# An MLP block on one core: where the sums of new weight blocks stand in superblock 1, and another fixed order for the first and last pair of later first matmuls

## The chip, the core and the metric

The kernel runs on one core of a Trainium2 chip. The core has a matrix engine (TensorE, "PE" in the profile; its weight loads are shown apart as "PEld"), a vector engine (VectorE, "DVE"), a scalar engine (ScalarE, "ACT"), a general engine (GpSimd, "POOL") and a sync engine (SyncE, "SP") that here issues DMA transfers. Each engine works through its own queue in order, and the engines wait for each other by semaphores. The metric is the device time of one execution in microseconds; less is better. Three runs of the kernel before gave 1500.38, 1503.52 and 1505.25 us.

## The reference

```python
def setup_inputs():
    batch, seq_len, hidden_dim = 8, 1024, 1024
    intermediate_dim = 4 * hidden_dim
    ...

def reference(x, w1, w2):
    h = x @ w1
    h = 0.5 * h * (1 + np.tanh(np.sqrt(2 / np.pi) * (h + 0.044715 * h ** 3)))
    return (h @ w2).astype(np.float32)
```

x has 8192 rows of 1024, w1 is 1024 x 4096, w2 is 4096 x 1024, all float32; the kernel multiplies in float16 and accumulates in float32.

## The kernel before

**Superblocks and matmuls.** The 8192 rows are taken in eight superblocks of 1024. Each has a first matmul (x times w1, then GELU, into g) and a second one (g times w2, into the output). Both use Strassen's scheme in Winograd's form: each operand is cut into four quarters, and seven products of quarters or of sums of quarters take the place of eight. The sums of the weights are `W_SUM` (numbers 5, 6, 7, 4; numbers 1, 2, 3 are plain quarters), the sums of the other operand `S_SUM`. From superblock 2 on some of the seven products are themselves cut once more in the same way; those are called inner products, and their sums inner sums.

**What superblocks 0 and 1 do besides.** w1 is worked on in four blocks ("quads", class `MadeQuad`) of two pairs each. Superblock 0 reads the weights, casts them and keeps the plain blocks in memory. Superblock 1 reads a plain block back (four loads of 512 KB on SP's queue, L201), makes its four sums on DVE (`sum`, L236) and stores each on POOL's queue (L246), and makes the inner sums of products 1 and 2 (`STORED_1`; four jobs each, `inner_jobs`, L252, stored at L270). It also makes the inner sums ("splits") of two products of the second matmul's w2 (`split_in_m1`, L1124: two loads on SP at L1130, four sums on DVE, four stores of 256 KB on POOL at L1141). Superblocks 2 to 7 only read all this back (`StoredHalf`, L296; loads at L318), except for the inner sums of products 3 and 5, which POOL makes (`make_sums`, L320, L329).

**The first matmul, `matmul1_seeded` (L754).** It runs over eight pairs of column chunks, j = 0 to 7. The order of all its work is written out by hand in tables: each entry is an operation and a number, its due place in thousandths of a pair; the entries of all pairs are merged by 1000 j + number (L946) and given out in that order, which fixes the order on every engine. `ORDER_PLAIN` serves every pair of superblock 1, `ORDER_HEAD` the first, `ORDER_TAIL` the last and `ORDER` the other pairs of superblocks 2 to 7. The entries are:

- `Pmch` with m the product, c the chunk and h the half: an outer step, two matmuls of 512 columns; `Pmrk` is step k of an inner product, two matmuls of 256 columns (L825, L832; the matmul itself is L821).
- `a`, `b`, `p5`: copies on ACT out of a PSUM bank (`move`, L876). `w`, `v`: additions on DVE of the copy p5 to bank A. `acc_`, `q11_`, `q12_`, `q2x_`: additions on DVE that put an inner product's parts together and into a bank (`add`, L853). PE writes into that bank next, so it waits for them.
- `gbch`: GELU on ACT (L892). After both gelus of blocks 11 and 21 POOL subtracts them (L903).
- `J`: a slot for jobs on DVE. It has room 1.2, and takes jobs from the pair's list until their costs have used it up (L805).

**The jobs.** In superblock 1 `Two.__init__` fills the list with what `ahead(j)` returns and with the splits that were set aside for this pair. In superblocks 2 to 7 pair 0 has the inner sums of x (`xs.inner_jobs`, four jobs of cost 0.42 per product) for those of products 1, 5, 2, 3 that the second matmul before hasn't made: eight jobs in superblock 2, twelve in the others. The operands that a `StoredHalf` loads, and their order on SP's queue, follow the order in which the table names its products (`operands_of`, L285).

All DVE operations have the line L152 in the profile, ACT's copies L168. Tiles named u come from one pool of 26 buffers, gc from one of 4, ps are the eight PSUM banks.

Of the kernel before, what the change touches and what calls it, by code (L numbers as in the profile page):

```python
# [21 lines left out]
SUMS = tuple(W_SUM)  # L22
# [2 lines left out]
INNER_1 = (1, 5, 2, 3)  # L25
STORED_1 = (1, 2)
SPLIT_IN_M1 = (2, 3)
SPLIT_AT = (0, 2, 4, 6)


def slots(table):
# [30 lines left out]
def order(text):  # L62
    return [(int(n), o) for o, n in (token.split(":") for token in text.split())]
# [4 lines left out]
    P2c00:511 P2c10:513 P2c01:526 P3c10:550 J:556 P3c00:564 P3c01:616 J:672 P7c00:704 P7c10:715  # L68
    P7c01:777 P7c11:817 P2c11:825 P3c11:825 g120:841 v0:852 v1:858 P4c00:871 P4c01:877 g111:883 g220:894
    P4c10:900 g110:904 P4c11:908 g121:1064 g210:1076 g211:1145 g221:1725""")  # L70
ORDER_HEAD = order("""J:-1385 P1c10:-1332 P1c11:-1168 J:-1152 P1c00:-1041 P1c01:-1039 a1:-953 P2r5:-773 a0:-627 P2r1:-592
    P5c00:-480 P5c10:-400 P5c01:-302 P6c00:-240 P6c01:-196 J:-160 P6c10:-111 J:-106 p50:170 acc_2:211
    q11_2:227 P2r6:278 P5c11:303 J:330 P6c11:342 w0:343 P3c00:354 q12_2:356 J:405 P3c01:417 p51:429
    P2r7:431 w1:433 P2r3:468 g120:488 q2x_2:504 P7c00:540 P2r2:577 J:584 J:690 P7c01:737 v0:792 J:827
    P2r4:841 g110:853 P7c10:856 P7c11:865 P3c10:953 v1:954 P4c00:982 g111:1052 P3c11:1079 J:1130 J:1151
    P4c01:1171 J:1211 g121:1215 g210:1320 P4c10:1380 P4c11:1511 g220:1571 g211:1653 g221:1719""")
ORDER = order("""P1r5:-255 P1r1:-201 q11_1:-134 P1r2:-80 s5_1:-76 P1r6:-72 P5r5:-7 q12_1:6 P5r1:10 P1r7:18 P1r3:20
    q11_5:166 s5_5:184 P5r2:194 P5r6:195 q2x_1:195 P1r4:203 a0:204 P2r5:204 q12_5:225 P6c00:229 P5r7:236
    a1:249 P5r3:277 P2r1:284 P6c01:320 q2x_5:387 q11_2:393 P6c10:398 P2r6:398 P5r4:403 P2r2:404 P3r5:408
# [1 line left out]
    P7c01:644 P3r6:653 P2r3:677 q2x_2:677 P7c10:680 acc_3:712 q12_3:729 g110:805 P2r4:810 P7c11:818  # L81
    v0:828 P3r7:857 P3r2:908 q2x_3:914 P3r3:924 P4c00:952 g111:994 v1:1049 g120:1106 P4c01:1111
    P3r4:1166 g121:1208 P4c10:1329 g210:1333 P4c11:1490 g220:1512 g211:1541 g221:1555""")
ORDER_TAIL = order("""P1r5:-319 P1r1:-290 s5_1:-54 q11_1:-44 P1r6:-31 q12_1:-17 P5r5:58 P5r1:105 P1r7:121 q11_5:124
    P1r2:134 s5_5:187 q2x_1:198 P5r2:203 P1r3:253 P5r6:266 P1r4:310 P2r5:319 a0:321 q12_5:357 P5r7:372
    P2r1:376 P5r3:389 q2x_5:389 P6c00:390 a1:398 P6c01:414 P5r4:415 P6c10:420 P6c11:434 q11_2:475
    acc_2:477 p50:505 P3r5:508 P3r1:508 P2r6:519 p51:523 w0:559 P7c00:563 w1:569 q11_3:643 P7c01:650
    q12_2:660 P3r6:666 v0:679 P7c10:684 P2r2:705 acc_3:734 P3r2:742 P2r3:782 P7c11:814 P4c00:868
    q12_3:880 P2r7:918 P3r7:922 v1:989 q2x_3:1011 P4c01:1063 P4c10:1110 q2x_2:1124 P4c11:1186 P3r4:1299
    P3r3:1390 P2r4:1431 g220:1455 g110:1463 g221:1715 g210:1802 g211:1864 g121:1875 g111:1922 g120:2446""")  # L90


@with_exitstack
def kernel(
# [11 lines left out]
    _, I = w1.shape  # L106
    _, O = w2.shape
# [5 lines left out]
    NI = I // P // 2  # L113
    OH = O // 2
    NQ = HT // P
    QC = 4
# [637 lines left out]
    def matmul1_seeded(xs, sb, quads):  # L754
        g = {b: gp.tile([P, NI, HT], GT, name=f"g{b}") for b in ("11", "12", "21", "22")}
        plain = sb == 1
        npair = NI // 2
# [4 lines left out]
        splits = {}  # L762

        def table(j):
            if plain:
                return ORDER_PLAIN
            return ORDER_HEAD if j == 0 else ORDER_TAIL if j == npair - 1 else ORDER

        class Two:
            def __init__(self, j):  # L770
                self.j, self.cs = j, (2 * j, 2 * j + 1)
                names = [o for _, o in table(j)]
                self.left = len(names)
                self.inner = [m for m in range(1, 8) if f"P{m}r1" in names]
                self.banks, self.temp, self.z = {}, {}, {}
                self.jobs, self.done = [], set()
                if plain:
                    self.source = quads[j // 2]
                    self.jobs = ahead(j) + splits.pop(j, [])
                    return  # L780
                for i in range(len(quads), min(j + 3, npair)):
                    quads.append(StoredHalf(i, table(i)))
                self.source = quads[j]
                if j == 0:
                    quads[0].make_sums()
                if j < npair - 1:
                    quads[j + 1].make_sums()
                if j == 0:
                    for m in INNER_1:
                        if m not in xs.inner:  # L790
                            pool = (gcp, "gc") if m in (1, 5) else (up, "u")
                            self.jobs += [(0.42, job) for job in xs.inner_jobs(m, *pool)]
# [119 lines left out]
        def ahead(j):  # L912

            q, second = divmod(j, 2)
            jobs = []
            if j < 2:
                jobs += quads[0].inner_jobs(STORED_1[j])
            if j in SPLIT_AT:
                i = SPLIT_AT.index(j)
                splits[j + 1] = [(0.7, job) for job in split_in_m1(SPLIT_IN_M1[i // 2], i % 2)]  # L920
            if q == NI // QC - 1:
                return jobs
            if not second:
                quads.append(MadeQuad(q + 1, False, True))
            quad = quads[q + 1]
            jobs += [(1.2, lambda m=m: quad.sum(m, pin=True)) for m in ((7, 4) if second else (5, 6))]
            jobs += quad.inner_jobs(STORED_1[second])
            return jobs

        def steady(j):  # L930

# [46 lines left out]
    def matmul2_made(sb, g, keep_w1, xb):  # L978
# [98 lines left out]
        for m, name, first in (  # L1077
# [3 lines left out]
            for q in range(NQ):  # L1081
# [12 lines left out]
                if (m, q) == (4, 0) and sb:  # L1094
                    quad = StoredHalf(0, ORDER_HEAD)
                if (m, q) == (1, NQ - 1) and sb == 0:
# [27 lines left out]
    def split_in_m1(m, h):  # L1124

        raw, t = [], {}
        for k in range(2):
            raw.append(gcp.tile([P, 2, HALF], DT, name="gc"))
            q = 2 * k + h
            nc.sync.dma_start(out=flat(raw[k]), in_=stored(w2_d[q], raw2_d[q], m))  # L1130

        def make(i, n):
            u, op, v = W_SUM[n]
            if i % 2 == 0:
                t["two"] = gcp.tile([P, 2, HALF], DT, name="gc")
            t[n] = t["two"][:, i % 2]
            in0, in1 = (
                t[b] if isinstance(b, int) else raw[int(b[0]) - 1][:, int(b[1]) - 1] for b in (u, v)
            )
            tt(t[n], in0, in1, op, True)  # L1140
            nc.gpsimd.dma_start(  # L1141
                out=in_d[m][:, i, h * QC:(h + 1) * QC, :].rearrange("p c n -> p (c n)"), in_=t[n]
            )

        return [lambda i=i, n=n: make(i, n) for i, n in enumerate(SUMS)]
# [175 lines left out]
    xs, quads = first.xs, [first.quad]  # L1321
    for sb in range(NSB):
# [4 lines left out]
        if sb < 2:  # L1327
            xs, quads = matmul2_made(sb, g, None if sb else quads[-1].keep_raw, nxt)
            continue
        matmul2(sb, g, early, nxt)  # L1330
        if nxt is not None:
            xs, quads = nxt, [StoredHalf(0, ORDER_HEAD)]

# [29 lines left out]
```

## Time and profile before

| | |
|---|---|
| median of three runs | 1503.52 us (1500.38 to 1505.25) |
| the profiled execution | 1499.09 us; its span 1497.3 us |
| granted TensorE clock, mean | 0.994 |
| first matmul of superblock 1 | from 208.50 to 315.57 us |
| its second matmul | to 412.27 us |
| first matmul of superblock 2 | from 412.27 to 503.21 us |
| its second matmul | to 588.86 us |
| first matmul of superblock 3 | from 588.86 to 682.60 us |
| DMA traffic | 452.23 MB, mean 302 GB/s |

The span is what lies between the first and the last instruction of the profiled execution. A line of the timeline gives the start and the length in us, the engine and source line, the operation, what it writes and reads, its tile, how many instructions were merged, and in brackets how long the engine had been idle before and what ended that. "issue" is time in which an engine waited for nothing that the profile shows. The ends of matmuls are modelled, since they are pipelined.

### The profile page before, as it was taken

Reading aid. Unit: us, or ns where it says so; the run is one execution under the profiler, and the core shown is the slowest. Engines: PE = TensorE matmul, PEld = TensorE weight load, DVE = VectorE, ACT = ScalarE, POOL = GpSimd, SP = SyncE. Lnnn points to the kernel's source line nnn. Section 1 sums busy time; section 2 is a strip of 40 time slices with the busy share of each in tenths; the row PEclk is TensorE's granted clock in tenths of the full one; section 3 lists DMA queues with packets and bytes.
Section 4 is the critical chain, followed back from the end, with each engine's and each line's share of the span. In section 5 each row is a group of like instructions: output and inputs, shape, how many; then the busy total and the mean of one; then the engine's idle time right before and its main releaser. Section 6 shows DMA issues by size and latency. Waiting matters only on the chain.

```text
span 1497.3 us, 27850 instructions
## 1 busy us (share of the span) xinstructions
PE 1467.9 (98%) x10347; PEld 1011.6 (68%) x10347; DVE 1169.4 (78%) x1672; ACT 606.7 (41%) x1210; POOL 560.1 (37%) x703
## 2 busy tenths in 40 slices
PE   8999989999999999999999999999999999999998
PEld 5444434444466787668866688666886678856787
DVE  5657348557867999779977799778997789877897
ACT  5665015531066411673126721267214662057510
POOL 2442124332377111861037611475115731157211
PEclk9999999999999999999999999999999999999999
DMA  9999898797897899969999699996999969996896
GB/s 324 339 360 404 203 383 293 261 316 250 332 288 211 271 349 351 333 186 362 351 321 305 169 371 337 357 276 198 391 299 352 275 190 378 324 350 215 301 310 198
DMA packets 241864, 452.23 MB, mean 302 GB/s; under 512 B 80576, under 2 KB 85696, under 8 KB 240832
## 3 DMA queue, kind: packets, MB, share of 16 engines
q1 hardware_dynamic: 214816, 357.12, 68.8%
q0 software_dynamic: 26912, 93.34, 21.1%
q8 instruction: 81, 1.33, 0.3%
q14 instruction: 55, 0.45, 0.1%
HBM read 353.89 MB, written 111.15 MB: 311 GB/s over the span
## 4 chain that ended last, share of the span: by engine, by line
PE 79%; DVE 4%; DMA 1%; issue 1%; SPq 0%; DVEq 0%
PE ps L821 40%; PE ps L1192 33%; PE ps L1233 6%; DVE u L152 2%; DMA u<-w_d 1%; DVE gc L152 1%; DVE tmp L152 0%; DVE ps L152 0%; SPq L318 0%; DVEq L152 0%
## 5 line engine op out<-in xcount | busy, mean ns | idle before, releaser
L821 PE MATMUL ps<-u 128*128 128x256 f16 (+1 forms) x3508 | 627.6, 328 | 20.4 <-DVE ps L152 20.4
L821 PEld LDWEIGHTS <-u 128*128 128x128 f16 x4180 | 411.2, 98 | 262.1 <-issue 33.7
L152 DVE TENSOR_TENSOR tmp<-tmp,ps 128x512 f32<-128x512 f32 x352 | 238.1, 685 | 127.6 <-PE ps L821 50.3
L1192 PE MATMUL ps<-u,gc 128*128 128x256 f16 x2688 | 300.3, 273 | 0.0
L168 ACT COPY tmp<-ps 128x512 f32<-128x512 f32 x282 | 163.8, 588 | 309.6 <-PE ps L821 150.8
L1192 PEld LDWEIGHTS <-gc 128*128 128x128 f16 x2688 | 262.9, 98 | 30.6 <-issue 0.2
L152 DVE TENSOR_TENSOR u<-u 128x2048 f16<-128x2048 f16 (+3 forms) x292 | 226.9, 818 | 26.4 <-DMA raw_d<-u 11.9
L892 ACT ACTIVATE g<-ps 128x512 f16<-128x512 f32 x336 | 197.9, 601 | 106.4 <-PE ps L821 105.8
L329 POOL TENSOR_TENSOR u<-u 128x256 f16<-128x256 f16 x336 | 216.4, 670 | 51.6 <-DMA u<-w_d 19.5
L1192 PE MATMUL ps<-u,g 128*128 128x256 f16 x2016 | 227.9, 273 | 0.0
L976 POOL DMA_DIRECT2D out_dram<-u x70 | 64.0, 960 | 432.0 <-DVE u L152 231.3
L168 ACT COPY u<-ps 128x512 f32<-128x512 f32 (+1 forms) x134 | 78.0, 587 | 347.2 <-PE ps L1192 340.4
L1192 PEld LDWEIGHTS <-g 128*128 128x128 f16 x2016 | 197.3, 98 | 22.8
L152 DVE TENSOR_TENSOR ps<-tmp,ps 128x256 f32<-128x256 f32 (+1 forms) x298 | 154.7, 532 | 38.4 <-PE ps L821 30.8
L903 POOL TENSOR_TENSOR g<-g,g 128x1024 f16<-128x1024 f16 x56 | 122.0, 2179 | 159.2 <-ACT g L892 159.1
L152 DVE TENSOR_TENSOR u<-u,ps 128x512 f32<-128x512 f32 x216 | 147.7, 684 | 36.5 <-PE ps L1192 27.9
L1233 PE MATMUL ps<-u,g 128*128 128x512 f16 x768 | 166.4, 379 | 0.0
L152 DVE TENSOR_TENSOR ps<-seed,ps 128x256 f32<-128x256 f32 (+1 forms) x168 | 94.5, 563 | 71.7 <-PE ps L821 69.3
L1233 PEld LDWEIGHTS <-g 128*128 128x128 f16 x768 | 75.1, 98 | 90.7
L821 PE MATMUL ps<-gc,u 128*128 128x256 f16 x672 | 120.4, 273 | 0.0
L152 DVE TENSOR_TENSOR gc<-g,gc 128x2048 f16<-128x2048 f16 x84 | 114.0, 1357 | 3.1 <-PE ps L1192 3.1
L152 DVE TENSOR_TENSOR gc<-g 128x2048 f16<-128x2048 f16 x78 | 95.1, 1220 | 0.0
(50 smaller groups left out, 741.6 us busy)
## 6 DMA issues: line engine op xcount, KB each, us to landing
u<-w_d SPq DMA_DIRECT2D x336, 256.0 KB, 6.6
u<-in_d SPq DMA_DIRECT2D x168, 512.0 KB, 7.9
u<-raw_d SPq DMA_DIRECT2D x252, 256.0 KB, 6.9
out_dram<-u POOLq DMA_DIRECT2D x70, 512.0 KB, 9.4
gc<-in_w_dram SPq DMA_DIRECT2D x48, 512.0 KB, 6.0
u<-in_d SPq DMA_DIRECT2D x90, 256.0 KB, 6.3
raw_d<-u SPq DMA_DIRECT2D x32, 512.0 KB, 8.5
u<-raw_d SPq DMA_DIRECT2D x32, 512.0 KB, 13.4
```

Source lines behind the costliest of these rows:

```text
L152: i = nc.vector.tensor_tensor(out=out, in0=in0, in1=in1, op=op)
L168: tc.keep_in_program_order(nc.scalar.copy(out=out, in_=in_))
L329: tc.keep_in_program_order(nc.gpsimd.tensor_tensor(out=operand(j), in0=operand(u), in1=operand(v), op=op))
L821: tc.keep_in_program_order(nc.tensor.matmul(out, lhsT=w, rhs=x, start=first, stop=True, skip_group_check=not first,))
L892: gelu_last[0] = nc.scalar.activation(out=g[b][:, self.cs[h], :], in_=src, func=GELU)
L903: nc.gpsimd.tensor_tensor(out=g["21"][:, cs], in0=g["11"][:, cs], in1=g["21"][:, cs], op=SUB)
L976: return nc.gpsimd.dma_start(out=rows, in_=src, **kw)
L1192: tc.keep_in_program_order(nc.tensor.matmul(bank[:, i * OH // 2:(i + 1) * OH // 2], lhsT=t[:, c, i * P:(i + 1) * P], rhs=self.y[j][:, c, : ...
L1233: tc.keep_in_program_order(nc.tensor.matmul(pair(bank), lhsT=a[:, c, :], rhs=chunks(pieces[c // QC])[:, :, c % QC, :], start=(first and c ...
```

## The change

Two things change. First, in superblock 1 the jobs are handed out differently. Before, pair j of a quad q made two of the four sums of the next quad (5 and 6 in the first pair, 7 and 4 in the second) and the inner sums of one stored product of it, and pairs 0 and 1 also made those of quad 0. After, the first pair of quad q makes the eight inner jobs of quad q itself (cost 0.8 each, so two to a slot), and the second pair makes all four sums of the next quad (one to a slot). The plain blocks are still loaded at the first pair of the quad before. The splits of w2 are loaded in pairs 1, 3, 5, 7 instead of 0, 2, 4, 6; they are made one pair after their load, and the last ones in pair 7 itself, where five empty jobs fill the five slots before them.

Second, `ORDER_HEAD` and `ORDER_TAIL` are other tables with the same operations, except that the head has four slots J instead of eleven, all of them late.

```diff
-SPLIT_AT = (0, 2, 4, 6)
+SPLIT_AT = (1, 3, 5, 7)
...
-ORDER_HEAD = order("""J:-1385 P1c10:-1332 P1c11:-1168 J:-1152 P1c00:-1041 P1c01:-1039 a1:-953 P2r5:-773 a0:-627 P2r1:-592
-    P5c00:-480 P5c10:-400 P5c01:-302 P6c00:-240 P6c01:-196 J:-160 P6c10:-111 J:-106 p50:170 acc_2:211
-    q11_2:227 P2r6:278 P5c11:303 J:330 P6c11:342 w0:343 P3c00:354 q12_2:356 J:405 P3c01:417 p51:429
-    P2r7:431 w1:433 P2r3:468 g120:488 q2x_2:504 P7c00:540 P2r2:577 J:584 J:690 P7c01:737 v0:792 J:827
-    P2r4:841 g110:853 P7c10:856 P7c11:865 P3c10:953 v1:954 P4c00:982 g111:1052 P3c11:1079 J:1130 J:1151
-    P4c01:1171 J:1211 g121:1215 g210:1320 P4c10:1380 P4c11:1511 g220:1571 g211:1653 g221:1719""")
+ORDER_HEAD = order("""P5c00:-1464 P2r5:-1229 P2r1:-1036 P1c10:-843 P1c11:-781 P1c00:-759 a1:-684 P1c01:-618 P5c10:-615
+    P5c01:-608 a0:-563 P5c11:-508 p50:-437 P6c10:-298 p51:-221 P6c11:-112 q11_2:-26 acc_2:-10 P6c00:41
+    w1:296 P2r6:411 P6c01:431 q12_2:466 P7c10:480 w0:511 P2r7:512 P7c11:542 q2x_2:548 v1:569 P2r2:622
+    P3c00:627 P2r3:640 J:652 g110:726 P2r4:745 P7c00:762 g221:778 P7c01:783 v0:785 P3c01:806 P4c10:833
+    J:913 P4c11:924 g111:937 P4c00:1006 P3c10:1017 P3c11:1026 g120:1046 g220:1078 J:1129 P4c01:1202
+    g121:1207 g210:1229 J:1337 g211:1528""")
...
-ORDER_TAIL = order("""P1r5:-319 P1r1:-290 s5_1:-54 q11_1:-44 P1r6:-31 q12_1:-17 P5r5:58 P5r1:105 P1r7:121 q11_5:124
...
-    q12_3:880 P2r7:918 P3r7:922 v1:989 q2x_3:1011 P4c01:1063 P4c10:1110 q2x_2:1124 P4c11:1186 P3r4:1299
-    P3r3:1390 P2r4:1431 g220:1455 g110:1463 g221:1715 g210:1802 g211:1864 g121:1875 g111:1922 g120:2446""")
+ORDER_TAIL = order("""P1r5:-249 P1r1:-200 s5_1:-147 q11_1:-70 P1r6:-70 q12_1:-37 P5r5:13 P5r1:48 P1r7:111 s5_5:170
...
+    P7c11:927 P7c01:954 P3r2:1060 v1:1155 P3r3:1164 g111:1166 v0:1218 P3r7:1237 P4c10:1247 g221:1254
+    g220:1306 P4c11:1309 g120:1341 P4c00:1667 q2x_3:1799 P4c01:1874 g211:1889 P3r4:1926 g210:2235
+    g121:2960""")
...
             q, second = divmod(j, 2)
             jobs = []
-            if j < 2:
-                jobs += quads[0].inner_jobs(STORED_1[j])
             if j in SPLIT_AT:
                 i = SPLIT_AT.index(j)
                 splits[j + 1] = [(0.7, job) for job in split_in_m1(SPLIT_IN_M1[i // 2], i % 2)]
-            if q == NI // QC - 1:
-                return jobs
-            if not second:
+                if j == npair - 1:
+                    return [(1.2, lambda: None)] * 5 + splits[j + 1]
+            if second:
+                return [(1.2, lambda m=m: quads[q + 1].sum(m, pin=True)) for m in SUMS]
+            if q < NI // QC - 1:
                 quads.append(MadeQuad(q + 1, False, True))
-            quad = quads[q + 1]
-            jobs += [(1.2, lambda m=m: quad.sum(m, pin=True)) for m in ((7, 4) if second else (5, 6))]
-            jobs += quad.inner_jobs(STORED_1[second])
-            return jobs
+            return [(0.8, job) for m in STORED_1 for _, job in quads[q].inner_jobs(m)]
```

More of the change, by code (lines that the diff above doesn't have):

```diff
@@ L83 @@
     P3r4:1166 g121:1208 P4c10:1329 g210:1333 P4c11:1490 g220:1512 g211:1541 g221:1555""")
-ORDER_TAIL = order("""P1r5:-319 P1r1:-290 s5_1:-54 q11_1:-44 P1r6:-31 q12_1:-17 P5r5:58 P5r1:105 P1r7:121 q11_5:124
[L85 to L88, printed above, removed]
-    q12_3:880 P2r7:918 P3r7:922 v1:989 q2x_3:1011 P4c01:1063 P4c10:1110 q2x_2:1124 P4c11:1186 P3r4:1299
-    P3r3:1390 P2r4:1431 g220:1455 g110:1463 g221:1715 g210:1802 g211:1864 g121:1875 g111:1922 g120:2446""")
+ORDER_TAIL = order("""P1r5:-249 P1r1:-200 s5_1:-147 q11_1:-70 P1r6:-70 q12_1:-37 P5r5:13 P5r1:48 P1r7:111 s5_5:170
+    P1r3:186 q11_5:191 q2x_1:209 P1r2:216 P5r6:218 P2r5:225 P2r1:270 P1r4:291 q12_5:307 a0:319 P5r7:331
+    P6c00:371 q2x_5:375 a1:376 q11_2:384 P5r2:392 P5r3:438 P6c01:448 acc_2:453 P5r4:479 P6c10:479
+    p50:496 P2r6:504 p51:517 P6c11:517 P3r5:527 w0:544 P3r1:560 q12_2:563 P2r3:565 P2r7:567 w1:635
+    P7c00:669 P2r2:712 q11_3:712 P3r6:779 P7c10:785 q2x_2:793 P2r4:883 g110:885 acc_3:902 q12_3:921
+    P7c11:927 P7c01:954 P3r2:1060 v1:1155 P3r3:1164 g111:1166 v0:1218 P3r7:1237 P4c10:1247 g221:1254
+    g220:1306 P4c11:1309 g120:1341 P4c00:1667 q2x_3:1799 P4c01:1874 g211:1889 P3r4:1926 g210:2235
+    g121:2960""")
 @with_exitstack
```

## The prediction

> **What bounds the kernel now.** I read the share of busy time first, then the chain of waits, then PE's timeline for gaps, then the table by stage. Busy times and the chain:
>
> ```profile
> PE 1467.9 (98%) x10347; PEld 1011.6 (68%) x10347; DVE 1169.4 (78%) x1672; ACT 606.7 (41%) x1210; POOL 560.1 (37%) x703
> PE 79%; DVE 4%; DMA 1%; issue 1%; SPq 0%; DVEq 0%
> ```
>
> PE sets the end, so only PE's gaps and PE's slow stretches can be won or lost. PE's timeline (start, length, instructions, in brackets the idle time before and its releaser) has gaps in two kinds of place:
>
> ```profile
> 219.76 13.93 PE L821 MATMUL ps<-u 128*128 128x512 f16 x56 [4.62 <-DVE ps L152]
> 234.85 24.50 PE L821 MATMUL ps<-u 128*128 128x512 f16 x112 [1.16 <-DVE ps L152]
> ...
> 596.34 3.62 PE L821 MATMUL ps<-u 128*128 128x256 f16 x20 [2.57 <-DVE ps L152]
> ...
> 775.68 5.31 PE L821 MATMUL ps<-u 128*128 128x256 f16 x20 [2.57 <-DVE ps L152]
> ```
>
> The first two lie in the first matmul of superblock 1, the others at the head (first pair) of superblocks 3 and 4; superblocks 5, 6, 7 repeat the last. The same 20 matmuls took 3.62 us after one gap and 5.31 after the other: a slow clock, 1.69 us on top. The table by stage for first matmuls, superblocks 2, 3, 4, 1 (length, busy PE, PEld, DVE, ACT, POOL, clock, DMA):
>
> ```profile
> 412.27:503.21 90.94, 90.94 (x624) 60.85 (x622) 67.44 (x121) 61.11 (x122) 59.61 (x77) 1.00 0.78 232
> 588.86:682.60 93.74, 91.17 (x624) 60.86 (x622) 73.53 (x136) 60.48 (x121) 60.27 (x78) 1.00 0.87 276
> 768.20:863.55 95.35, 92.78 (x624) 61.33 (x622) 73.70 (x136) 60.53 (x121) 60.27 (x78) 0.98 0.85 266
> ...
> 208.50:315.57 107.07, 99.50 (x449) 44.23 (x448) 65.35 (x88) 50.40 (x94) 38.54 (x53) 0.98 0.85 313
> ```
>
> Superblock 2 has no gap: 90.94 is the floor. Against it superblock 3 loses 2.80 and 4 to 7 lose 4.41 each (95.35, 95.35, 95.34, 95.35): 20.4 us in all. In superblock 1 ACT's copies of operation b start every 12.09 us where nothing is late; from 209.57 to 304.61 seven pairs took 95.04, against 84.63: 10.4 us lost, 6.5 of it in pair 0.
>
> Why DVE is late, in its own timeline: superblock 1's pair 0, its pair 3, and the head of superblock 3.
>
> ```profile
> 213.60 1.23 DVE L152 TENSOR_TENSOR u<-u 128x2048 f16<-128x2048 f16 x1 [6.37 <-DMA u<-raw_d]
> ...
> 251.09 5.96 DVE L152 TENSOR_TENSOR u<-u 128x2048 f16<-128x2048 f16 x6
> 256.98 2.61 DVE L152 TENSOR_TENSOR gc<-gc 128x1024 f16<-128x1024 f16 x4
> ...
> 593.80 1.55 DVE L152 TENSOR_TENSOR u<-u 128x512 f16<-128x512 f16 x4
> 595.27 0.68 DVE L152 TENSOR_TENSOR tmp<-tmp,ps 128x512 f32<-128x512 f32 x1
> 595.86 1.02 DVE L152 TENSOR_TENSOR ps<-tmp,ps 128x256 f32<-128x256 f32 x2
> ```
>
> In pair 0 a sum of the new block waits for its load, with the addition w that PE needs queued behind it. In pair 3 eight jobs fill DVE before w. At the head the twelve jobs (590.87 to 595.27, 4.4 us) stand in front of the additions acc_2 and q11_2 that PE waits for.
>
> **The change, superblock 1 (expected -10.4 us).** Pair 0 loses the two sums of block 1 and gets the eight inner jobs of block 0, whose operands are on the chip: four of them ran by 207.2, four more take 1.55 us, so DVE is free by 209; w is due about 213. The wait for the load goes. What is late next is that sum itself, now one pair (12.09 us) later; the load landed at 213.6, so not late. Later pairs before w: an even one now has eight inner jobs (3.1 us) and two splits (half of 2.61); an odd one four sums (2.35 for two, so 4.7). To both I add the 2.2 us that DVE stood still in pair 3 while POOL's L903 ran (254.29 to 256.42, no load missing): 6.6 and 6.9 us. Before, pair 3 took 8.3 from the end of v (251.18) to w (259.50) and PE lost 1.2; pair 4 took 6.1 (264.40 to 270.49) and lost nothing. So the limit is near 7.1 and both fit, by 0.2 at the narrowest; if that cover is gone, three odd pairs cost up to 1 us each.
>
> Every moved job carries its store: four 512 KB stores now stand on POOL's queue in the odd pair with L903 behind the third, about 4 us after v. Nothing of PE waits for L903 before the second matmul. The last splits move into pair 7: their two loads wait on SP's queue for the splits of pair 6, and the sixteen w2 loads of the second matmul queue behind them. Those began at 285.41, 30 us ahead of use; now about 18. The first four need some 8 us to land, so I cost this at nothing; a landing over 14 us would hold up v in pair 7 and PE with it. On POOL the last two x casts stand behind the four split stores; they are read 27 us later. Bounds: 0 and -10.4; I take -10.4.
>
> **The change, heads of superblocks 2 to 7.** The head begins with P5, P2r5, P2r1, and all its J slots stand late (652, 913, 1129, 1337). Taken out: the 20.4 us above, since acc_2 and q11_2 now stand ahead of the jobs. P5c00 needs the first load of its half block and P1 the fourth instead of the first; the fourth was issued at 578.57 and took 7.1 us to land, 3 us before the head began at 588.86: no cost. Given back: each group of three jobs now has a nearby reader on PE. From the end of P2r7 DVE needs q2x_2, v1 (0.60 each, v1 after P7c11) and one job of 0.42, about 1.75 us with latencies; PE gets to P1r5 in 1.5 (P7c11 0.43, P2r2 0.22, P3c00 0.43, P2r3 and P2r4 0.43). So about 0.3 us is late at the first group even undisturbed. PE reaches the first group 7.8 us after the head's start (15 outer steps of 0.432 and six parts of 0.217), the others at some 11, 13 and 16 us. And there is company:
>
> ```profile
> 599.14 2.66 POOL L329 TENSOR_TENSOR u<-u 128x256 f16<-128x256 f16 x4 [8.30 <-DMA u<-w_d]
> ```
>
> POOL's sixteen L329 sums began 10.3 us after the head's start and lasted till 22.3; in superblock 2 from 1.6 to 12.8. In the old order no job ran beside them, so what that costs is not in the trace. From below: nothing. From above, by L903's row, a job waits out a whole L329 (0.67). Once per later group: 0.3 + 3 x 0.67 = 2.3 us a head. I take 1.6, nearer the upper end as three of four groups meet L329: six heads give back 9.6. Ends 1.8 and 13.8.
>
> Here the Trainium skill speaks against the change ("SBUF — State Buffer", section "SBUF: two separate sides"): DVE and GpSimd share one port pair, an exclusive lock held for a whole instruction. Pair 3's row agrees. Read strictly, every one of the twelve jobs may meet an L329; that sum is the slower rival's, by the trace's own 0.67.
>
> **Tails.** The last pair's new order puts P4c00, P4c01, P3r4 and three gelus last. PE had no gap there nor at the turn to the second matmul, which begins with 12 us on g22, whose gelus (g220, g221) now stand earlier. Cost nothing; without that cover, three gelus at 0.6, 1.8 us on each of six tails.
>
> **Sum.** -10.4 - 20.4 + 9.6 = -21.2 us. The profiled execution took 1499.09 us (span 1497.3), so 1477.9; the median of the runs, 1503.52, lies 4.4 above it, and I put the forecast there: 1482.3.
>
> **Rivals.** (a) Slower: the port decides. If each of the twelve jobs waits out an L329, a head is late by 8.0 us (5.4 with eight jobs in superblock 2): 45.4 given back against 30.8 won, 1518. It decides from 5.1 us a head. For: DVE is 76% busy in steady pairs (51.77 of 68), so a backlog drains slowly. Against: POOL's own waits for loads leave holes, and both sides queue, so one wait a job is the most. (b) The heads' gap only moves: a wait over 2.5 us in pair 1, with the slow clock behind it, 4.4 us on all six heads. Then -10.4 + 6 x 4.4 - 20.4 = -4.4: 1499; with half of that 1490. For: the row at 599.14. Against: the groups are spread, and gaps of 1.16 and 0.89 left the clock alone (24.50 us for 112 matmuls). (c) Superblock 1 doesn't gain, because sums or splits still meet late loads (landing there took 14.0 us in the median): 1493. Against: every load has a pair more.
>
> **How the numbers follow.** Main case 0.70 (1474 to 1490), (b) 0.14, (a) 0.09, (c) 0.05, something unseen 0.02. The bottom is -10.4 - 20.4 + 1.8 = -29.0, 1474.5; the top takes in (c) and most of (b): 1474 to 1497. A change under 0.3% (4.5 us) can't be told from none. Faster: main, (c) and 0.10 of (b), 0.85; within 0.3%: 0.05; slower: 0.10.
>
> **What would show it.** Right: no gap over 0.3 us in superblock 1's first matmul and pairs of 12.09 us; no 2.57 us gap at the heads, gaps under 1 us 8 to 16 us after their start released by DVE's gc or ps, clock 1.00. Wrong: DVE jobs interleaved with L329 at twice their 0.42 us, a gap over 2.5 us in pair 1, a gap at the turn to the second matmul.

## The result, and the profile after

The changed kernel takes 1495.32 us in the median of 20 executions, against 1502.22 us for 20 of the kernel before: a ratio of 0.9952, 95% interval 0.9937 to 0.9968, so 6.9 us faster. The forecast was 21.2 us faster. The direction held; two thirds of the gain are missing. The values also scatter: 1488.07 to 1501.81 us after, 1499.74 to 1505.25 before. The profiled execution of the changed kernel took 1501.35 us (span 1499.6), one of its slowest; the profiled one of before, 1499.09 us, was faster than each of the 20. So the two profiles show which stages won and lost, and the experiments have to say how much of it is in every execution.

Line numbers move by one or two: DVE's operations are L153 now, the first matmul's L822, POOL's sums L330, the loads in order L166. Busy times and the chain of waits:

```profile
PE 1467.4 (98%) x10347; PEld 1010.3 (67%) x10347; DVE 1178.6 (79%) x1672; ACT 604.0 (40%) x1210; POOL 569.5 (38%) x703
PE 21%; DMA 3%; DVE 1%; POOL 0%; issue 0%; SPq 0%; ACT 0%; POOLq 0%; DVEq 0%
```

The table by stage (window, length, busy PE, PEld, DVE, ACT, POOL, clock, DMA share, GB/s): superblock 1's first and second matmul, then the first matmuls of superblocks 2, 3 and 4, and for comparison superblock 1's second matmul in the kernel before:

```profile
209.16:305.86 96.70, 96.70 (x450) 43.84 (x448) 62.79 (x93) 50.37 (x94) 41.47 (x56) 1.00 0.86 309
305.86:416.02 110.16, 99.34 (x450) 44.39 (x449) 65.04 (x80) 10.41 (x19) 28.75 (x52) 0.94 1.13 267
416.02:508.61 92.59, 91.77 (x624) 60.68 (x622) 74.09 (x134) 61.20 (x124) 60.60 (x77) 1.00 0.84 261
594.20:689.05 94.85, 91.89 (x624) 60.70 (x622) 76.22 (x136) 60.72 (x123) 61.28 (x78) 1.00 0.87 272
774.64:869.41 94.77, 91.90 (x625) 60.65 (x623) 76.08 (x136) 60.73 (x123) 61.20 (x78) 1.00 0.84 267
```

```profile
315.57:412.27 96.70, 96.70 (x450) 43.83 (x449) 69.67 (x92) 10.42 (x19) 28.94 (x52) 1.00 0.85 285
```

The chain, followed back, covers only about a quarter of the span here, so the stages are read from the table. Three things are to be seen. Superblock 1's first matmul runs without a gap, 96.70 us against 107.07: the 10.4 us are there. Its second matmul took 96.70 us before and takes 110.16 now: 13.5 us are gone again, 10.8 in one gap and 2.6 in a slower clock (0.94) behind it. And the heads, where the forecast had 10.8 us, give almost nothing: the six first matmuls add up to 565.60 us against 566.08.

PE's timeline has the gap, and the gaps at the head of superblock 3:

```profile
410.08 6.10 PE L1231 MATMUL ps<-u,g 128*128 128x512 f16 x16 [10.82 <-DVE tmp L153]
...
602.65 0.38 PE L822 MATMUL ps<-gc,u 128*128 128x256 f16 x2 [0.29 <-DVE gc L153]
...
607.15 0.39 PE L822 MATMUL ps<-gc,u 128*128 128x256 f16 x2 [1.31 <-POOL u L330]
...
611.02 0.38 PE L822 MATMUL ps<-gc,u 128*128 128x256 f16 x2 [0.66 <-DVE ps L153]
...
614.23 0.38 PE L822 MATMUL ps<-u 128*128 128x256 f16 x2 [0.67 <-DVE ps L153]
```

Where the 10.82 us come from is read backwards, first in DVE's timeline:

```profile
320.51 1.23 DVE L153 TENSOR_TENSOR u<-u 128x2048 f16<-128x2048 f16 x1 [9.91 <-DMA u<-raw_d]
...
407.00 2.43 DVE L153 TENSOR_TENSOR u<-u 128x2048 f16<-128x2048 f16 x3 [20.83 <-DMA u<-xb]
```

DVE waits 20.83 us for the transposed x of the next superblock, with the additions that PE needs queued behind. Then in SP's queue, after and before (start, length, DMAs issued):

```profile
288.45 1.26 SPq L1128 DMA_DIRECT2D gc<-raw_d  x2
289.81 29.72 SPq L166 DMA_DIRECT2D u<-raw_d  x16
320.57 71.57 SPq L166 DMA_TRANSPOSE u<-xb  x16
```

```profile
284.39 0.92 SPq L1130 DMA_DIRECT2D gc<-raw_d  x2
285.41 22.57 SPq L165 DMA_DIRECT2D u<-raw_d  x16
326.04 28.85 SPq L165 DMA_TRANSPOSE u<-xb  x16
```

The sixteen w2 loads start 4.4 us later and take 7 us longer, though the second matmul begins 9.7 us earlier. The transposes follow right behind them, and issuing them takes 71.57 us instead of 28.85. Between 318 and 393 us a transpose took 20.8 us from issue to landing in the median (4.4 before), and POOL's stores of 512 KB 14.7 to 15.5 (4.5 before).

### The profile page after: what moved, and what is told of

Read it like the earlier page. It is cut to its first block, busy times and chain, and to the rows that moved or that the text cites. A ratio compares the mean times of both kernels' runs of the same rounds, so it can differ in the third digit from the quotient of the medians.

```text
span 1499.6 us, 27809 instructions
## 1 busy us (share of the span) xinstructions
PE 1467.4 (98%) x10347; PEld 1010.3 (67%) x10347; DVE 1178.6 (79%) x1672; ACT 604.0 (40%) x1210; POOL 569.5 (38%) x703
## 5 line engine op out<-in xcount | busy, mean ns | idle before, releaser
L822 PE MATMUL ps<-u 128*128 128x256 f16 (+1 forms) x3508 | 621.0, 325 | 3.3 <-DVE ps L153 3.0
L822 PEld LDWEIGHTS <-u 128*128 128x128 f16 x4180 | 408.0, 98 | 254.6 <-issue 16.5
L153 DVE TENSOR_TENSOR tmp<-tmp,ps 128x512 f32<-128x512 f32 x352 | 237.1, 684 | 92.1 <-PE ps L822 35.5
L153 DVE TENSOR_TENSOR u<-u 128x2048 f16<-128x2048 f16 (+3 forms) x292 | 224.6, 811 | 64.3 <-DMA u<-xb 20.8
L330 POOL TENSOR_TENSOR u<-u 128x256 f16<-128x256 f16 x336 | 222.4, 687 | 54.9 <-DMA u<-in_d 15.8
L153 DVE TENSOR_TENSOR ps<-tmp,ps 128x256 f32<-128x256 f32 (+1 forms) x298 | 155.4, 532 | 40.1 <-PE ps L822 26.4
L904 POOL TENSOR_TENSOR g<-g,g 128x1024 f16<-128x1024 f16 x56 | 125.8, 2246 | 147.3 <-ACT g L893 140.4
L1231 PE MATMUL ps<-u,g 128*128 128x512 f16 x768 | 169.1, 383 | 10.8 <-DVE tmp L153 10.8
L153 DVE TENSOR_TENSOR u<-u,ps 128x512 f32<-128x512 f32 x216 | 148.0, 685 | 36.5 <-PE ps L1190 27.9
L153 DVE TENSOR_TENSOR ps<-seed,ps 128x256 f32<-128x256 f32 (+1 forms) x168 | 93.8, 561 | 59.4 <-PE ps L822 52.0
L822 PE MATMUL ps<-gc,u 128*128 128x256 f16 x672 | 123.4, 273 | 10.8 <-DVE ps L153 4.8
L153 DVE TENSOR_TENSOR gc<-g,gc 128x2048 f16<-128x2048 f16 x84 | 114.2, 1359 | 4.1 <-PE ps L1190 3.1
L153 DVE TENSOR_TENSOR gc<-g 128x2048 f16<-128x2048 f16 x78 | 95.2, 1221 | 1.2 <-PE ps L1190 1.2
## 6 DMA issues: line engine op xcount, KB each, us to landing
raw_d<-u SPq DMA_DIRECT2D x32, 512.0 KB, 10.1
```

The costliest lines, as they stand in the source:

```text
L153: i = nc.vector.tensor_tensor(out=out, in0=in0, in1=in1, op=op)
L330: tc.keep_in_program_order(nc.gpsimd.tensor_tensor(out=operand(j), in0=operand(u), in1=operand(v), op=op))
L822: tc.keep_in_program_order(nc.tensor.matmul(out, lhsT=w, rhs=x, start=first, stop=True, skip_group_check=not first,))
L904: nc.gpsimd.tensor_tensor(out=g["21"][:, cs], in0=g["11"][:, cs], in1=g["21"][:, cs], op=SUB)
L1231: tc.keep_in_program_order(nc.tensor.matmul(pair(bank), lhsT=a[:, c, :], rhs=chunks(pieces[c // QC])[:, :, c % QC, :], start=(first and c ...
```

## The experiments

Theory W: superblock 1's gain is real, and a varying part of it is lost in its second matmul, because w2 loads and transposes of x now meet there. Rival H: the spread comes from the heads. The first four kernels separate the two halves of the change.

**Superblock 1 alone**: the old `ORDER_HEAD` and `ORDER_TAIL` are put back.

```diff
-ORDER_HEAD = order("""P5c00:-1464 P2r5:-1229 ...
+ORDER_HEAD = order("""J:-1385 P1c10:-1332 ...
...
-ORDER_TAIL = order("""P1r5:-249 P1r1:-200 ...
+ORDER_TAIL = order("""P1r5:-319 P1r1:-290 ...
```

> Superblock 1 as changed, the old head and tail. In the profiled execution of the changed kernel its first matmul took 96.70 us against 107.07 (10.4 won), and its second 110.16 against 96.70 (13.5 lost, 10.8 of it one gap). Theory W (the gap comes from superblock 1's new order, and its size differs from execution to execution): times spread from about 1489 (no gap) to about 1504 (the full one), the median 2 to 8 us under the kernel before. Rival H (the spread comes from the new heads): times as tight as those of the kernel before, 10 us under it, and no gap in the second matmul.

Measured: 1493.52 us (1490.75 to 1500.02), ratio 0.9944 (0.9923 to 0.9966). The spread is there without the new heads; the transposes took 61.62 us to issue. In the profiled execution (1492.22 us) PE had no gap in the second matmul: the slow transposes are there each time, the gap is not. Superblock 2's first matmul, whose loads queue behind the transposes, took 93.01 us against 90.94 before, with waits for a load (0.56) and for POOL's sums (1.16).

**The tables alone**: the kernel before, with the changed tables.

```diff
-ORDER_HEAD = order("""J:-1385 P1c10:-1332 ...
+ORDER_HEAD = order("""P5c00:-1464 P2r5:-1229 ...
...
-ORDER_TAIL = order("""P1r5:-319 P1r1:-290 ...
+ORDER_TAIL = order("""P1r5:-249 P1r1:-200 ...
```

> The old superblock 1, the new head and tail. Added up over six heads, the first matmuls of the profiled executions differ by only 0.5 us (20.4 taken out, 19.9 given back). Theory W with heads that are worth nothing: within 2 us of the kernel before, and as tight as it; no gap in superblock 1's second matmul. Rival H: the spread of 14 us is here. By the prediction's own sum (1.6 given back per head) it would be 10.8 under the kernel before.

Measured: 1501.07 us (1499.17 to 1503.14), ratio 0.9988 (0.9978 to 0.9997): 1.2 us won, no spread. The new heads are worth 1.2 us, not 10.8. H falls.

**Splits early again**, sums where the change puts them:

```diff
-SPLIT_AT = (1, 3, 5, 7)
+SPLIT_AT = (0, 2, 4, 6)
...
-                if j == npair - 1:
-                    return [(1.2, lambda: None)] * 5 + splits[j + 1]
+            if j == npair - 1:
+                return [(1.2, lambda: None)] * 5
```

> The changed kernel with the splits of w2 loaded in pairs 0, 2, 4, 6 and made in pairs 1, 3, 5, 7, as before the change; the sums stay where the change puts them. Theory S (the last splits' loads and stores in pair 7 are what holds up the second matmul): the gap at 410 us goes, about 1489 and tight. Rival M (the moved sums of w1 and their stores are enough): a gap before superblock 2 remains and the spread with it, the median within 3 us of the changed kernel's. The odd pairs now hold four sums and four splits on DVE, which may cost up to 1 us each in superblock 1's first matmul.

Measured: 1490.81 us (1488.73 to 1492.52). No gap, and the six times lie within 3.8 us. SP's queue has the loads ten microseconds earlier and quick transposes:

```profile
278.74 0.92 SPq L1128 DMA_DIRECT2D gc<-raw_d  x2
279.76 24.84 SPq L166 DMA_DIRECT2D u<-raw_d  x16
319.60 27.28 SPq L166 DMA_TRANSPOSE u<-xb  x16
```

It costs 2.2 us in superblock 1's first matmul (98.90 us): the odd pairs are too full for DVE, as expected.

**The changed kernel again**, for a second profile.

> The changed kernel unchanged, for a second profiled execution. Theory W: the time moves with superblock 1's second matmul alone: a time of T goes with a second matmul of about 96.7 + (T - 1488) us, and the heads' 94.4 to 94.9 us stay. Rival H: the heads' lengths differ and the second matmul keeps its 110 us.

Measured: five of six executions at 1489.60 to 1491.77 us, one at 1499.77. The profiled one (1491.29 us) had a second matmul of 96.69 us, 13.5 less than in the first profile. The first matmuls of superblocks 2 to 7 took 93.9 to 95.6 us, in sum 2.6 more, where Theory W had them stay. So the time that this execution won lies in that one stage. The transposes were slow here too, 59.25 us, but DVE's wait for them ended at 392.57 instead of 407.00, just in time. Why they took 12 us longer in the first profile isn't shown. The stage's row, then DVE's:

```profile
305.59:402.28 96.69, 96.69 (x449) 43.83 (x448) 65.69 (x82) 10.41 (x19) 27.18 (x49) 1.00 1.12 282
...
392.57 2.43 DVE L153 TENSOR_TENSOR u<-u 128x2048 f16<-128x2048 f16 x3 [6.67 <-DMA u<-xb]
```

The next two were to separate the late loads from the start of the transposes, by an order hint behind another engine's instruction. Neither start moved (318.24 us against 318.61 in the second profile of the changed kernel, 279.67 against 279.76 with early splits). So they decide nothing between the theories named in their expectations, and count as repeats of these two kernels.

```diff
+                if (m, q) == (2, 0):
+                    at["hold"] = i
...
-                    xs = XOps(x_transpose(xb, load_in_order))
+                    if sb:
+                        with tc.issue_after(at["hold"].ins):
+                            xs = XOps(x_transpose(xb, load_in_order))
...
```

> The changed kernel; the sixteen transposes of x may start only after DVE's first addition of the second matmul's second product (328.46 us in the profiled execution of the changed kernel, where they started at 320.57). Theory T (what slows the transposes is that they start together with the stores of the late w2 sums): started at about 329 they take some 28 us and land in 5 to 6 us, as in the kernel before, and PE has no gap at 410 us. Rival L (the w2 sums come 10 us late and so their stores bunch; when the transposes start does not matter): they still take 55 to 70 us and land in 17 to 21 us, and they end 8 us later than before, so PE's gap stays or grows.

Measured: 1490.25 us, a single execution; transposes from 318.24 us, slow as ever (60.46 us).

```diff
+                    if plain and self.j == npair - 2:
+                        hold[1] = hold[0]
...
-                    load_in_order(flat(t), raw2_d[q][:, BLOCKS.index(b), :])
+                    with tc.issue_after(hold[1].ins):
+                        load_in_order(flat(t), raw2_d[q][:, BLOCKS.index(b), :])
```

> The kernel with the early splits, which had no gap and 5.7 us to land a transpose; here the sixteen w2 loads are held back until pair 6's copy p5, so that they begin at about 288.5 us, as in the changed kernel, instead of 279.8. The order and the amount of everything else stay. If the late w2 loads alone are the cause: transposes take 55 to 70 us and land in 17 to 21 us again, the times spread over 1490 to 1504 us. If it is the splits' own stores or loads in pair 7: transposes as quick as with the early splits, times of 1489 to 1493.

Measured: 1490.50 us (1489.87 to 1491.31); loads from 279.67 us, transposes quick (26.68 us).

For a hold that holds, a small transfer that reads the result waited for was put on SP's queue:

```diff
+    hold = dram.tile([P, 8], F32, name="hold")
...
                     act_copy(self.tmp("p5")[:, h], self.bank("C", h))
+                    if plain and self.j == npair - 2 and h == 1:
+                        load_in_order(hold, self.tmp("p5")[:, h, :8])
```

> The last try to hold the loads back left their start at 279.7 us, so it held nothing; here a 4 KB transfer of pair 6's copy p5 stands on SP's queue ahead of the sixteen w2 loads of the kernel with the early splits, so that they begin at about 288.5 us as in the changed kernel. If the late w2 loads alone are the cause: DVE's first sum of w2 at 318 to 321 us instead of some 311, transposes of 55 to 70 us in all that land in 17 to 21 us, times spread over 1490 to 1504. If the splits of pair 7 are the cause by themselves: transposes of 27 us, landing in 5 to 6, times of 1489 to 1493.

Measured: 1489.98 us (1489.18 to 1490.71). Early splits, loads held to 287.92 us: the transposes are slow again.

```profile
287.50 0.32 SPq L168 DMA_DIRECT2D hold<-tmp  x1
287.92 19.29 SPq L168 DMA_DIRECT2D u<-raw_d  x16
320.10 56.78 SPq L168 DMA_TRANSPOSE u<-xb  x16
```

So later w2 loads are enough to slow the transposes, with the splits as early as in the kernel whose transposes are quick. Two parts of the expectation missed: the times aren't spread, and DVE's first sum of w2 came at 312.07 us, in time; only a later one waited (1.85 us, at 321.04). So late sums of w2 aren't needed for it. The four times are tight and the profiled one has no gap: the slow transposes were made again, the gap was not.

**The other way round**: the changed kernel with its late loads, and the transposes held.

```diff
+                if sb and (m, q) == (2, 0):
+                    load_in_order(hold, t[:, :8])
                 at[q] = store(sb, {2: "11", 3: "12", 7: "22"}[m], q, t)
```

> The changed kernel, with a 4 KB transfer of the result of DVE's first addition of the second product ahead of the transposes on SP's queue: the earlier try left them at 318.24 us, here they start at 326 to 329, some 8 us after the first w2 sum (7.4 in the kernel with early splits, 1.5 or less in the changed one). Theory T (it is the start together with the w2 sums' stores): transposes of 27 to 30 us, landing in 5 to 6, times tight at 1488 to 1492. Rival L (the bunched stores of the whole stretch): 55 to 70 us, landing in 17 to 21, the end of the transposes later by 8, PE's gap more often: times of 1490 to 1505.

Measured: 1489.22 us (1488.08 to 1490.46), ratio 0.9919 (0.9902 to 0.9935), no gap.

```profile
326.14 0.32 SPq L168 DMA_DIRECT2D hold<-tmp  x1
326.68 28.64 SPq L168 DMA_TRANSPOSE u<-xb  x16
```

Started 8 us later they ended 22 us earlier than the unheld ones of the second profile. DVE's first sum of w2 was late here too, by 7.60 us (8.22 in that profile), and its store was issued at 319.0 us (320.1 there), so rival L falls: late sums and bunched stores aren't enough. DVE no longer waits for the transposed x; its sums begin at 385.37 us. The four tight times alone would say little, since five of six of the unheld kernel were under 1492 too. What the kernels have in common shows when the landing of the last w2 load (its issue plus its time to landing) is set against the start of the transposes:

| kernel | last w2 load landed | transposes start | overlap | their issue took | median to landing |
|---|---|---|---|---|---|
| before | 327.4 | 326.04 | 1.4 | 28.85 | 4.4 |
| transposes held | 327.6 | 326.68 | 0.9 | 28.64 | 6.7 |
| splits early | 325.5 | 319.60 | 5.9 | 27.28 | 5.7 |
| early splits, loads held | 329.2 | 320.10 | 9.1 | 56.78 | 17.9 |
| changed, second profile | 328.7 | 318.61 | 10.1 | 59.25 | 18.7 |
| changed, first profile | 331.5 | 320.57 | 10.9 | 71.57 | 20.8 |
| superblock 1 alone | 329.1 | 317.66 | 11.4 | 61.62 | 18.1 |

The other seven profiles agree: six with an overlap of 0.9 to 5.5 us took 26.52 to 28.06 us, the repeat of the changed kernel with 11.6 us took 60.46. Up to 5.9 us of overlap the transposes are quick, from 9.1 on slow; no profile lies between. A landing is itself later where the two meet, so the table alone would prove little; but the two held kernels move one end each, and each switches between quick and slow. Why they then stay slow long after the last load has landed isn't shown.

**The heads.** POOL's sums for pair 1 are left out in the kernel with early splits; plain quarters are multiplied in their place, so the outputs of that pair are other ones. They are eight, not sixteen as the expectation says: POOL makes 48 sums in superblock 3 instead of 56, and the next eight, for pair 2, begin 19.7 us after the head's start, when the head's jobs on DVE are done.

```diff
-                if j < npair - 1:
+                if 0 < j < npair - 1:
                     quads[j + 1].make_sums()
...
-                    if r in S_TERM:
-                        a, b = (int(d) - 1 for d in S_TERM[r])
+                    if r in S_TERM or (self.j == 1 and m not in STORED_1):
+                        a, b = (int(d) - 1 for d in S_TERM.get(r, "11"))
```

> The kernel with the early splits; POOL makes no inner weight sums for pair 1 of superblocks 2 to 7, and PE multiplies plain quarters there instead, so the outputs of that pair are other ones; PE has the same matmuls. The sixteen POOL sums at the heads are gone. Theory P (a job of DVE takes twice its 0.42 us while one of POOL's sums runs, nearly every job, and PE also waits for those sums): jobs of 0.42 us, first matmuls at 91.2 to 91.9 us instead of 94.1 to 95.4, the time 15 to 19 us shorter, 1472 to 1476. Rival Q (DVE has too much to do at the head whoever runs beside it): jobs of 0.42 us but gaps on PE of over 2 us remain, 1485 to 1490.

Measured: 1480.93 us in a single execution, 9.5 under the profiled one with the sums; the six first matmuls add up to 555.69 us against 565.92. Between the two expectations: the sums cost 1.7 us a head in the mean (nothing in superblock 2, with 92.61 and 92.71 us, and 2.1 in each of the others), and as much again is lost without them. DVE's jobs show it, in the changed kernel and then with the sums left out (the fifth and sixth job of superblock 3's head; in the changed kernel also the addition behind them):

```profile
604.87 0.89 DVE L153 TENSOR_TENSOR gc<-u 128x512 f16<-128x512 f16 x1
605.79 0.77 DVE L153 TENSOR_TENSOR gc<-u,gc 128x512 f16<-128x512 f16 x1
606.49 0.42 DVE L153 TENSOR_TENSOR ps<-seed,ps 128x256 f32<-128x256 f32 x1
```

```profile
594.03 0.42 DVE L153 TENSOR_TENSOR gc<-u 128x512 f16<-128x512 f16 x1
594.49 0.43 DVE L153 TENSOR_TENSOR gc<-u,gc 128x512 f16<-128x512 f16 x1
```

POOL's first sums in that head of the changed kernel, the company of those jobs:

```profile
604.80 6.09 POOL L330 TENSOR_TENSOR u<-u 128x256 f16<-128x256 f16 x8 [8.62 <-DMA u<-w_d]
```

From the fifth job on, eight of the twelve took 2.7 us longer in all than without the sums, and POOL's own took 0.76 us each instead of 0.67. The addition at 606.49, which reads a PSUM bank, took 0.42 us beside the sums, and 0.43 without them. POOL began only when a load had landed, and PE waited 1.31 us for the sums themselves; in the five heads with early splits these waits were 0.50 to 1.64 us. How much of the 1.7 us is DVE's longer jobs and how much PE's waits isn't separated.

**An early slot**: three jobs go to the very start of the head, where DVE stands idle, still with early splits. (The old head had twelve slots, the changed one has four.)

```diff
-ORDER_HEAD = order("""P5c00:-1464 ...
+ORDER_HEAD = order("""J:-1465 P5c00:-1464 ...
...
-                            self.jobs += [(0.42, job) for job in xs.inner_jobs(m, *pool)]
+                            self.jobs += [(1.2 if m == 5 and i == 3 else 0.42, job) for i, job in enumerate(xs.inner_jobs(m, *pool))]
```

> The kernel with the early splits, and a fifth slot J at the very start of the head, where DVE stands 1.3 us idle and POOL has no sum to run: three of the jobs move there, the others move up. Theory P: three jobs fewer meet POOL's sums, and the first group is ready in time: 0.28 + 3 x 0.42 = 1.5 us a head, 8 to 9 us in all, 1482 us. Rival Q: the additions acc_2 and q11_2 come 1.3 us later and PE waits for them: 1490 or more.

Measured: 1491.18 us (1488.77 to 1492.73), nothing won. Neither expectation: the first gap is gone and the additions at the start aren't late, but a larger one opens further on, of which DVE's and PE's timelines show why:

```profile
595.54 2.29 DVE L153 TENSOR_TENSOR u<-u 128x512 f16<-128x512 f16 x3 [2.50 <-PE ps L822]
```

```profile
598.49 0.38 PE L822 MATMUL ps<-gc,u 128*128 128x256 f16 x2 [2.12 <-DVE ps L153]
```

The jobs have moved up, those of product 3 now stand ahead of q12_5 and q2x_1, and wait for a buffer that PE still reads. So the slot at 1129 was put behind those additions, to 1230.

> The kernel with the early slot, its slot 1129 moved to 1230, behind the additions q12_5 and q2x_1 of pair 1. With the early slot alone PE's gap at those additions grew to 1.45 to 2.76 us, since three jobs that waited for a buffer stood ahead of them on DVE. If that order was what the early slot gave back: this gap falls under 0.7 us, first matmuls of 92.8 to 93.6 us instead of 94.4 to 97.4, the time 1481 to 1485. If POOL's sums decide (PE waits 0.65 to 1.64 for them, and DVE's jobs and additions take twice as long beside them): 94 us or more remain, 1488 to 1491.

Measured: 1486.31 us (1485.60 to 1487.53), ratio 0.9898 (0.9883 to 0.9912), first matmuls of 92.3 to 95.0 us. Half of what was expected: the gap at those additions fell under 0.7 us in three heads and stayed at 1.12 to 1.50 in the other three, and PE's waits for POOL's sums remain (0.83 to 1.66).

**Both repairs in one**: late splits with the transposes held, and this head.

> The changed kernel's superblock 1 (late splits, whose first matmul ran at 96.69 us against 98.9 with early ones) with the transposes held behind DVE's first addition of the second product, and the heads with the early slot and slot 1230. If the two halves add up: transposes of some 28 us that land in about 6, no gap in superblock 1's second matmul, and 2.2 us under the last kernel's 1486.31: 1483 to 1485, tight. If the transposes and the new heads disturb each other, or the hold is not enough in every execution: a spread of over 5 us, or a median of 1486 or more.

Measured: 1483.23 us (1482.12 to 1484.36), ratio 0.9873 (0.9857 to 0.9890): faster than both kernels, by 18.8 us against the one before. Transposes 26.52 us, no gap in superblock 1, the six first matmuls 558.61 us in all.

## Why the prediction was right, and where it was not

**Superblock 1's first matmul: right.** -10.4 was forecast, -10.4 is there in every profile of the changed kernel: no gap, eight pairs in 96.70 us. The margins came out differently. From the end of v DVE was busy for 4.7 us in an odd pair (6.9 forecast), since L903, now L904, starts only at 224.09 us in pair 1, when the last sum is already running, and for 6.1 us in an even one (6.6 forecast). With the splits back in the odd pairs 2.2 us are lost.

**The w2 loads: wrong, and this is one of the two steps that failed.** The prediction put it so: "the sixteen w2 loads of the second matmul queue behind them. Those began at 285.41, 30 us ahead of use; now about 18. The first four need some 8 us to land, so I cost this at nothing". For PE's first four loads the cost was nothing, but with luck: they took 9.0 to 13.7 us to land in the kernel before, not 8, and in the changed kernel the fourth landed 0.2 us (first profile) and 1.5 us (second) before the second matmul began. The other twelve were not followed, nor what stands behind them on the same queue. The sum of w2 that DVE makes first needs the ninth load, and was late by 9.91 us in the first profile; above all the transposes of x are next on SP, and started 10 to 11 us before the last load had landed. In the kernel before SP had waited 17.9 us for the cast x ahead of them; with the stage 9.7 us earlier at most 1.3 us of that wait are left, while the loads come later. The overlap doubled the time of the transposes. Some executions had room for it and some did not: the two profiles lost 0 and 13.5 us. With the transposes held, the same kernel takes 1489.22 us, 13.1 under the kernel before; as it is, 6.9 under. Following SP's queue past the loads would have met the transposes.

**The x casts: right.** They land in time; SP waited 1.3 us for them in the second profile and not in the first.

**The heads: the mechanism was right, the size wrong; this is the other step that failed.** Taken out were 20.4 us, as forecast: no gap of 2.57 us is left and the clock is 1.00. Given back were "0.3 + 3 x 0.67 = 2.3 us a head. I take 1.6"; measured are 565.60 less six times 90.94, 19.96 us, so 3.3 a head, above the upper bound. Without POOL's sums a head still loses (555.69 - 545.64) / 6 = 1.7 us, where the term for undisturbed work was 0.3, since it followed only the first group. That group's gap is there as forecast (0.29 us in superblock 3), but a second one of 0.25 to 1.12 us opens at additions of pair 1, and PE is busy 0.67 us longer than the floor (91.61 against 90.94 in superblocks 3 and 4), of which the cause isn't shown. POOL's sums add 1.7 (I had 1.3): not one job a group but eight of twelve meet one, at up to twice their 0.42 us, the sign named beforehand for "wrong"; and PE waits for the sums themselves, which no term had. The reading of the loads at the head was off too, at no cost: the row at 578.57 holds the third and the fourth, and the fourth landed at 587.7, 1.2 us before the head and not 3. The Trainium skill's rule of the shared port pair ("SBUF — State Buffer", "SBUF: two separate sides"), held for a whole instruction, agrees with 0.42 us alone and 0.77 to 0.89 beside a sum.

**Tails: right.** The second matmuls after them take 85.59 us as before.

**Rivals.** (a), twelve jobs that each wait out 0.67 us, priced a head at 8.0 us: far too high: eight wait 0.3 us in the mean and four not at all. (b), a gap of over 2.5 us in pair 1 with the slow clock behind it, didn't come; its time was nearly right for another reason. Half of its gap makes 1486 (-10.4 + 13.2 - 20.4 = -17.6) and not the 1490 of the prediction. (c) falls with superblock 1. No rival looked at superblock 1's second matmul. That 1495.32 still lies below the top of 1497 is luck: the top was set for (b) and (c), and neither came; the main case, 1474 to 1490, missed.

**The sum.** -10.4 in superblock 1 held; -10.8 at the heads became -1.2; and 10.4 + 1.2 - 6.9 = 4.7 us are left to the median, which I put down to the second matmul and what its slow transposes delay; in a single execution that stage took back nothing or 13.5.

## What to carry to other kernels

When work is moved past a queue, follow that queue to its end: the first transfers behind it may have time to spare and the last ones not. When a median has moved but the runs scatter more, profile the same kernel twice: the stage that differs is where to look. And when jobs are spread out to close one gap, look at the due time of each job's own reader and at what runs beside it on the other engine, not only for the first group.

## What was not expected of the hardware

Transposes that started 9.1 us or more before the last w2 load on the same queue had landed were slow as a whole, and so was what ran beside them: the 512 KB stores took 14.7 to 15.5 us to land in the first profile of the changed kernel, instead of 4.5. Between 318 and 393 us the DMA engines were busy throughout in that profile, but moved 239 GB/s in the mean and for up to 9 us on end under 100; with the transposes held they moved 317 GB/s, and in the kernel before 256, with pauses. The sixteen transposes, 2 MB, took 26.5 to 28.9 us to issue in nine profiles and 56.8 to 71.6 in five, nothing between; in the other superblocks of the same profiles they took 20.9 to 23.1 us. The Trainium skill says that transposes are as fast as other transfers and expects 350 to 400 GB/s ("Advanced Engine Details and Errata", "X-Bar Transpose (TRN2)"); beside other traffic they ran here at 29 to 79 GB/s, 2.1 MB over those times. That is the rate at which SP issued them; no run here shows how fast such transfers are with nothing beside them.
